# The even mixer's scan re-ordered: fronts in three pinned steps, single-step preparations, Toeplitz blocks in column tiles, and a warm-up of seven matmuls

## The chip, the cores and the metric

The kernel runs on one core of one Trainium2 chip, in one launch. The metric is the device time of a launch in microseconds; the median of several runs is compared. Times within the profile are microseconds from the start of the profiled execution, unless marked ns.

## The reference, cut to what matters

One inference step of a two-layer encoder for 512 prompt frames and 32 sample frames. Layer 0 has the even mixer, which the change is in; layer 1 (attention and gated MLP) and both convolutional feed-forward blocks are untouched.

```python
z = hn @ w_even_in                       # 1024 -> 3*512 + 512
gb, gc, xa, u = split(z)
ya = gb * causal_dwconv(gc * xa)         # part A, three taps
# part B: 32 groups of 16 channels, each with 64 complex states
bu = einsum(u, bb)                       # input into the states
hs = scan(h[t] = ab * h[t-1] + bu[t])    # complex diagonal recurrence
yb = real(einsum(hs, c)) + d * u         # states to channels, skip term
g  = gelu(yb)
yb = g * sigmoid(g @ w_glu)
y  = concat(ya, yb) @ w_even_out
```

## The kernel before

All large products are done in fp32r with each operand split into a high and a low part, so that one product is three matmuls (L131 to L133): `mm_job` issues 24 of them for one tile of 128 output columns and one half of the frames (256 or 288 columns). Weights come as 512 KB tiles: SP loads `raw` (L106), ACT makes the high part `wh` (L107), VectorE the low part `wl` (L108).

The even mixer is `mixer_even`. Its stages in order: the input norm; four tiles of the projection for `u` (evicted by `c_u`); a shuffle of `u` by 16 DMAs on SP, from frames into blocks of four frames (`UU` to `U4`, L924); then the phase of the other twelve projection tiles (`c_a`: gate, convolution input and taps, into `ya`), beside which part B runs; after it the glu (96 matmuls on `GG`), and the output projection.

Part B works on blocks of four frames, with 137 columns (`M`) for both groups of requests. Each of eight *fronts* `front(s)` takes two of the 16 state tiles: the matmuls `v` put the input into the states, VectorE rotates them with the table `E` (`rt`, then two `rg`), ACT writes the decay `cv` into a part of `sp` (L872), VectorE runs the scan (L875), rotates back (`rt`, L877) and writes the states into `sp` (L878, L879). `back(s)` multiplies the states by `Cm` (L891) and adds the products within a block through the Toeplitz blocks `Tm` (L893); ACT's gelu (L894) writes the result over `U4`. `shuffle(True, ...)` takes it back to frames, also on SP (L924). The tiles `rt`, `rg`, `sp` and `G` share four buffers (tag "pt"), so a front needs buffers that earlier fronts, backs or preparations have released. `GG` takes the buffer of `E`.

The tables are prepared meanwhile: `prep_g(ch)` makes the input table `Bm` for a chunk of four state tiles (VectorE products `gt`, ACT copies into `G`, transposes `tb`, ACT copies); `prep_c()` makes `Cm` in five portions `tau` (VectorE products, ACT copies, L794) and then zeroes `Tm`; `prep_t(ch)` makes the blocks of `Tm`: eight matmuls `tp` into 32 partitions (L837), evicted by ACT and, for the first block with the skip term `d`, by four VectorE steps (L842), and three SP DMAs (L845) that copy the block row to the other three partition groups.

The order is set by generators: `task(scan())` hands `scan`'s steps to `phase`, which after each projection tile takes two of them (`rate=2`) while evictions lag two tiles behind. Each engine then executes its instructions in the order written, except where the scheduler moves one whose operands are late; SP's loads and DMAs stand in one queue.

At the very start a warm-up of nine fp32 matmuls on zeros (L218, two passes each) runs while the first operands arrive.

Of the kernel before, what the change touches and what calls it, by code (L numbers as in the profile page):

```python
# [24 lines left out]
M = 137  # L25
# [16 lines left out]
for _n, _w in (("g_mix_pre", 16), ("g_mix_post", 16), ("g_ffn_pre", 16), ("g_ffn_post", 16),  # L42
               ("conv_a", 12), ("hist_a", 8), ("a_re", 16), ("a_im", 16),
               ("log_dt", 16), ("st_re", 16), ("st_im", 16), ("d", 16), ("b_forget", 1),
               ("g_gmlp", 4), ("conv_f", 264)):
    _pc(_n, _w)
NPRM = PC["_n"]
NPRM0 = PC["conv_f"][0]

NCST = 128 + 128 + 32  # L50

# [20 lines left out]
def trunk_kernel(ctx: ExitStack, tc: tile.TileContext, A: dict):  # L72
    nc = tc.nc
    vec, act, pool_e, pe = nc.vector, nc.scalar, nc.gpsimd, nc.tensor
# [141 lines left out]
    warm = mm.tile([128, 512], F32, tag="mm", name="warm")  # L216
    for _ in range(9):
        pe.matmul(warm[:, 0:256], zero[:, 0:1].to_broadcast([128, 128]), zero[:, 0:1].to_broadcast([128, 256]),  # L218
                  start=True, stop=True)
# [298 lines left out]
    def mixer_even(h):  # L518
        ms = ExitStack()
        s5 = ms.enter_context(tc.tile_pool(name="s5", bufs=1))  # L520
# [259 lines left out]
        def prep_c():  # L780
            ct = Tm.rearrange("p (n i a x) c -> p n i a (x c)", n=2, i=2, a=2)
            ct = ct.rearrange("p n i a (q c) -> p n i a q c", q=16)
            for tau in range(5):
                src = raw[:, 0]
                if tau:
                    t = ct[:, tau % 2]
                    for i in range(2):
                        p_ = pw[:, tau, i][:, None, :, None].to_broadcast([128, 2, 16, 16])
                        vec.tensor_tensor(t[:, i], raw[:, i], p_, op=OP.mult)
                    src = t[:, 0]  # L790
                    vec.tensor_tensor(src, src, t[:, 1], op=OP.add)
                for g in range(2):
                    s = slice(g * 64, g * 64 + 64)
                    act.activation(Cm[s, :, :, tau, g * 16:g * 16 + 16], src[s], AF.Copy)  # L794
                if tau % 2 == 0:
                    yield
            act.activation(Tm.rearrange("p q s -> p (q s)"), zero[:, 0:1].to_broadcast([128, 2048]), AF.Copy)
            yield

        g3 = {}  # L800

        def prep_g(ch):
            q0 = 4 * ch
# [9 lines left out]
            for i in range(2):  # L813
                p_ = pg[:, i, q0:q0 + 4][:, None, :, :, None].to_broadcast([128, 2, 4, 3, 16])
                b_ = bb[:, i, ch][:, :, :, None].to_broadcast([128, 2, 4, 3, 16])
                vec.tensor_tensor(t[i].rearrange("p (r q) j c -> p r q j c", r=2), b_, p_, op=OP.mult)
            vec.tensor_tensor(t[0], t[0], t[1], op=OP.add)
            for g in range(2):
                s = slice(g * 64, g * 64 + 64)
                o = G[s, :, :, 0:3, g * 16:g * 16 + 16].rearrange("p r q j c -> p (r q) j c")  # L820
                act.activation(o, t[0][s], AF.Copy)
            yield
            for r in range(2):
# [28 lines left out]
        def front(s):  # L852
# [13 lines left out]
            t4 = t.rearrange("p e r (q m) -> p e r q m", q=2)  # L866
            vec.tensor_tensor(t, v[:, None].to_broadcast([128, 2, 2, 2 * M]), e, op=OP.mult)
# [7 lines left out]
            vec.tensor_tensor_scan(g_[:, 1], cf, g_[:, 0], 0.0, op0=OP.mult, op1=OP.add)  # L875
            w_ = g_[:, 1].rearrange("p (r x) -> p r x", r=2)
            vec.tensor_tensor(t, w_[:, None].to_broadcast([128, 2, 2, 2 * M]), e, op=OP.mult)  # L877
            vec.tensor_tensor(sp[:, 0, :, 1:M + 1], t4[:, 0, 0], t4[:, 1, 1], op=OP.subtract)  # L878
            vec.tensor_tensor(sp[:, 1, :, 1:M + 1], t4[:, 0, 1], t4[:, 1, 0], op=OP.add)  # L879
# [496 lines left out]
def host_arrays(inp):  # L1376
# [142 lines left out]
```

## Time and profile before

| | before |
|---|---|
| median of 3 runs | 1392.94 us (1390.91 to 1394.11) |
| profiled execution | 1392.53 us |
| its span in the trace | 1390.8 us |
| TensorE busy | 1367.2 us, 98% |
| VectorE busy | 935.7 us, 67% |
| ScalarE (ACT) busy | 657.4 us, 47% |

The span is the part of the profiled execution that the trace shows; 1.7 us lie around it. Busy shares are means over stages that differ, so the stage of the change (28 to 156 us) is read by itself: how full each engine is there, what ended the waits of TensorE and VectorE, and in what order the last pieces of part B and of the projection come.

### The profile page before, as it was taken

How to read it: one execution, taken by the hardware profiler on the slowest of the kernel's cores; microseconds unless marked ns; L12 is line 12 of the kernel's file. 1: busy time of each engine (PE TensorE's matmuls, PEld its weight loads, DVE VectorE, ACT ScalarE, POOL GpSimd, SP SyncE). 2: the span in 40 equal slices, each digit the busy share in tenths (PEclk: the TensorE clock that was granted, in tenths of full speed). 3: DMA queues.
4: the chain of work that ended last, by engine and by line, in shares of the span. 5: the costliest groups of instructions: out<-in, count | busy, mean ns of one | idle time of the engine just before them, and what ended most of it. 6: DMA issues, size and time to landing. Idle time of an engine off the chain costs nothing.

```text
span 1390.8 us, 27437 instructions
## 1 busy us (share of the span) xinstructions
PE 1367.2 (98%) x10859; PEld 1344.2 (97%) x10859; DVE 935.7 (67%) x1968; ACT 657.4 (47%) x1314; POOL 198.3 (14%) x621
## 2 busy tenths in 40 slices
PE   8899999999999999999999999999999999999998
PEld 8798999999999999999998998999999999999998
DVE  9998738983477546868655555479843676368682
ACT  6653545543344223445547755465433343234451
POOL 1000000431022201300131100012320123013000
PEclk9999999999999999999999999999999999999999
DMA  6322352232312231331332332331223123313321
GB/s 199 94 67 63 117 184 77 77 96 72 122 62 86 97 122 39 105 113 53 99 94 70 117 109 64 108 107 62 92 92 122 46 92 107 99 50 94 100 73 50
DMA packets 49376, 128.26 MB, mean 92 GB/s; under 512 B 8368, under 2 KB 19896, under 8 KB 48992
## 3 DMA queue, kind: packets, MB, share of 16 engines
q1 hardware_dynamic: 47456, 124.35, 28.0%
q0 software_dynamic: 1792, 2.17, 0.7%
q8 instruction: 85, 1.39, 0.4%
q14 instruction: 43, 0.35, 0.1%
HBM read 116.93 MB, written 4.76 MB: 88 GB/s over the span
## 4 chain that ended last, share of the span: by engine, by line
PE 87%; DVE 8%; ACT 2%; SPq 1%; DMA 1%; issue 1%; POOL 0%; ACTq 0%; DVEq 0%
PE ps L131 27%; PE ps L133 27%; PE ps L132 27%; DVE wl L108 1%; SPq L924 1%; PE av L1254 1%; PE rp L307 1%; DVE Xl L327 1%; PE pp L1243 1%; DVE rg L875 1%; DVE rt L877 1%; ACT wh L107 1%; PE sc L1230 1%; DVE y L338 0%; DMA h<-in_x 0%
## 5 line engine op out<-in xcount | busy, mean ns | idle before, releaser
L131 PE MATMUL ps<-Xh,wh 128*128 128x256 f32 (+1 forms) x2512 | 728.1, 290 | 1.8 <-ACT wh L107 1.1
L133 PE MATMUL ps<-Xh,wl 128*128 128x256 f32 (+1 forms) x2512 | 725.5, 289 | 2.0 <-DVE wl L108 2.0
L132 PE MATMUL ps<-Xl,wh 128*128 128x256 f32 (+1 forms) x2512 | 725.6, 289 | 0.8 <-DVE Xl L327 0.5
L131 PEld LDWEIGHTS ps<-Xh,wh 128*128 128x128 f32 x2512 | 473.9, 189 | 4.4 <-ACT wh L107 1.6
L132 PEld LDWEIGHTS ps<-Xl,wh 128*128 128x128 f32 x2512 | 474.7, 189 | 3.0 <-DVE Xl L327 1.2
L133 PEld LDWEIGHTS ps<-Xh,wl 128*128 128x128 f32 x2512 | 473.0, 188 | 2.5 <-DVE wl L108 2.4
L108 DVE TENSOR_TENSOR wl<-raw,wh 128x1024 fp32r<-128x1024 f32 (+2 forms) x214 | 256.9, 1201 | 151.3 <-ACT wh L107 149.5
L107 ACT ACTIVATE wh<-raw 128x1024 fp32r<-128x1024 f32 (+2 forms) x214 | 222.1, 1039 | 248.3 <-PE ps L132 232.9
L131 PE MATMUL ps<-gh,wh 128*128 128x288 f32 (+1 forms) x704 | 203.5, 289 | 0.0
L133 PE MATMUL ps<-gh,wl 128*128 128x288 f32 (+1 forms) x704 | 203.4, 289 | 0.0
L132 PE MATMUL ps<-gl,wh 128*128 128x288 f32 (+1 forms) x704 | 202.5, 288 | 0.0
L132 PEld LDWEIGHTS ps<-gl,wh 128*128 128x128 f32 x704 | 133.5, 190 | 0.0
L131 PEld LDWEIGHTS ps<-gh,wh 128*128 128x128 f32 x704 | 133.0, 189 | 0.0
L133 PEld LDWEIGHTS ps<-gh,wl 128*128 128x128 f32 x704 | 132.9, 189 | 0.0
L278 ACT ACTIVATE t<-U,prm 128x256 f32<-128x256 f32 (+1 forms) x176 | 90.4, 517 | 71.0 <-DVE U L413 67.5
L279 DVE SCALAR_TENSOR_TENSOR t<-U,prm,t 128x256 f32<-128x256 f32 (+1 forms) x176 | 87.2, 498 | 34.9 <-ACT t L278 34.7
L413 DVE TENSOR_TENSOR U<-ps,rB 128x256 f32<-128x256 f32 (+1 forms) x176 | 76.6, 437 | 23.9 <-PE ps L133 19.8
L280 DVE SCALAR_TENSOR_TENSOR t<-U,prm,t 128x256 f32<-128x256 f32 (+1 forms) x176 | 87.5, 501 | 4.5
L416 POOL COPY hca<-U 128x2 f32<-128x2 f32 x88 | 24.3, 277 | 366.2 <-DVE U L413 366.1
L423 ACT ACTIVATE t<-t 128x288 f32<-128x288 f32 (+1 forms) x88 | 37.7, 429 | 81.6 <-DVE t L280 81.5
L439 DVE TENSOR_TENSOR y<-y,ps 128x256 f32<-128x256 f32 (+1 forms) x64 | 27.9, 436 | 62.0 <-PE ps L133 62.0
L429 ACT ACTIVATE gh<-t 128x288 fp32r<-128x288 f32 (+1 forms) x88 | 37.4, 425 | 67.3 <-DVE t L427 67.3
(272 smaller groups left out, 1376.7 us busy)
## 6 DMA issues: line engine op xcount, KB each, us to landing
raw<-in_w_up SPq DMA_DIRECT2D x88, 512.0 KB, 3.4
raw<-in_w_down SPq DMA_DIRECT2D x32, 512.0 KB, 3.4
raw<-in_w_odd_in SPq DMA_DIRECT2D x21, 512.0 KB, 3.6
raw<-in_w_gate SPq DMA_DIRECT2D x16, 512.0 KB, 4.0
raw<-in_w_even_in SPq DMA_DIRECT2D x15, 512.0 KB, 3.7
raw<-in_w_down SPq DMA_DIRECT2D x16, 384.0 KB, 3.1
raw<-in_w_even_out SPq DMA_DIRECT2D x8, 512.0 KB, 4.0
raw<-in_w_odd_out SPq DMA_DIRECT2D x8, 512.0 KB, 3.5
```

The costliest lines, as they stand in the source:

```text
L107: act.activation(wh[:, k], raw[:, k], AF.Copy)
L108: vec.tensor_tensor(wl[:, k], raw[:, k], wh[:, k], op=OP.subtract)
L131: pe.matmul(ps[:, :n], wh[:, k0 + k, :], h_, start=(i == 0), stop=False)
L132: pe.matmul(ps[:, :n], wh[:, k0 + k, :], l_, start=False, stop=False)
L133: pe.matmul(ps[:, :n], wl[:, k0 + k, :], h_, start=False, stop=(i == last))
L278: act.activation(t, v[2], AF.Copy, scale=w(2))
L279: vec.scalar_tensor_tensor(t, v[1], w(1), t, op0=OP.mult, op1=OP.add)
L280: vec.scalar_tensor_tensor(t, v[0], w(0), t, op0=OP.mult, op1=OP.add)
L413: vec.tensor_tensor(block_view(U, half)[2], like(ps, half), like(rB[half], half), op=OP.mult)
L423: act.activation(t, t, AF.Gelu_apprx_tanh)
L429: act.activation(gh[:, f - f0], g, AF.Copy)
L439: vec.tensor_tensor(yk, yk, ps, op=OP.add)
```

## The change

- The warm-up has 7 matmuls, not 9.
- `front` becomes three steps: up to `cv`; the scan and the second `rt`; the two `sp`. Its first product, the scan and the first `sp` step are pinned (`tc.keep_in_program_order`), so the scheduler keeps them where they are written, behind the evictions that were written earlier. The products of `prep_c` and `prep_g` are pinned too.
- `scan` takes the preparations from a list, one step at a time, one or two between the steps of the fronts. `prep_c` has one step for each `tau` and none of its own for the zeroing of `Tm`. `back(s - 2)` follows the scan step of front `s`; the shuffle of the first half is issued at `s == 6`; backs 6 and 7 come at the very end.
- `prep_t` puts its four matmul pairs into four column tiles of 32 columns, so that the block rows lie on 128 partitions; one VectorE step (with an identity stacked four times, `eye4`, and `d` in four columns) and one ACT copy evict them into a single buffer `ts`, and sixteen SP DMAs a chunk write `Tm`.
- The parameter table is 12 columns narrower and the constants 32 columns wider.

```diff
@@ prep_c, prep_g
-                        vec.tensor_tensor(t[:, i], raw[:, i], p_, op=OP.mult)
+                        pin(vec.tensor_tensor(t[:, i], raw[:, i], p_, op=OP.mult))
...
-                if tau % 2 == 0:
+                if tau:
                     yield
...
-            yield
+            yield True
@@ prep_t
-            for i in range(4):
-                for r in range(2):
-                    pe.matmul(ps[0:32, i * 128:i * 128 + 128], G[:, r, i],
-                              Cm[:, r, q0 + i, 0:4].rearrange("p t c -> p (t c)"), start=(r == 0), stop=(r == 1))
-            pv = ps[0:32].rearrange("p (q s) -> p q s", q=4)
-            act.activation(Tm[0:32, q0:q0 + 4, 32:128], pv[:, :, 32:128], AF.Copy)
-            for i in range(4):
-                vec.scalar_tensor_tensor(Tm[0:32, q0 + i, 0:32], ident[0:32, 0:32], P("d", q0 + i)[0:32],
-                                         pv[:, i, 0:32], op0=OP.mult, op1=OP.add)
-            for j in range(1, 4):
-                nc.sync.dma_start(Tm[j * 32:j * 32 + 32, q0:q0 + 4, j * 32:128], Tm[0:32, q0:q0 + 4, 0:128 - j * 32])
+            ts_ = s5.tile([128, 128], F32, tag="ts", name="ts")
+            for r in range(2):
+                for i in range(4):
+                    pe.matmul(ps[32 * i:32 * i + 32, 0:128], G[:, r, i],
+                              Cm[:, r, q0 + i, 0:4].rearrange("p t c -> p (t c)"), start=(r == 0), stop=(r == 1),
+                              tile_position=(0, 32 * i))
+            vec.scalar_tensor_tensor(ts_[:, 0:32], eye4, P("d", ch), ps[:, 0:32], op0=OP.mult, op1=OP.add)
+            act.activation(ts_[:, 32:128], ps[:, 32:128], AF.Copy)
+            for j in range(4):
+                for i in range(4):
+                    nc.sync.dma_start(Tm[j * 32:j * 32 + 32, q0 + i, j * 32:128],
+                                      ts_[32 * i:32 * i + 32, 0:128 - j * 32])
@@ scan
-            for s in range(10):
-                if s >= 2:
-                    back(s - 2)
-                    yield
-                if s == 5:
-                    shuffle(True, (0, 1))
-                if s < 8:
-                    front(s)
-                    yield
-                    if s == 0:
-                        yield from prep_c()
-                    if s % 2 == 0:
-                        yield from prep_t(s // 2)
-                    elif s < 5:
-                        yield from prep_g(s // 2 + 2)
+            side = [prep_c(), prep_t(0), prep_g(2), prep_t(1), prep_g(3), prep_t(2), prep_t(3)]
+            left = [0, 0, 1, 3, 5, 5, 6, 6]
...
+            for s in range(8):
+                while 7 - len(side) < left[s]:
+                    yield beside()
+                f = front(s)
+                next(f)
+                yield
+                yield beside()
+                next(f)
+                yield
                 if s >= 2:
                     back(s - 2)
-                    yield
...
+                x = beside()
+                if s == 6:
+                    shuffle(True, (0, 1))
+                yield x
+                next(f, None)
+                yield
+            while side:
+                beside()
+            back(6)
+            yield
+            back(7)
             shuffle(True, (2, 3))
```

Where the instructions stand now, at three places. The first is TensorE at the first chunk of `Tm`; `v` is the input of front 1 before and of front 2 now, `tp` the Toeplitz matmuls of chunk 0, `ps` a projection tile. Before:

```order
L133 MATMUL ps<-Xh,wl 128x288
L858 MATMUL v<-UUh,Bm 128x137 x4
L837 MATMUL tp<-Cm,g_707 32x128 x8
L131 MATMUL ps<-Xh,wh 128x256
L132 MATMUL ps<-Xl,wh 128x256
```

Changed:

```order
L133 MATMUL ps<-Xh,wl 128x288
L860 MATMUL v<-UUh,Bm 128x137 x3
L839 MATMUL tp<-Cm,g_705 32x128 x8
L860 MATMUL v<-UUh,Bm 128x137
L131 MATMUL ps<-Xh,wh 128x256
```

`tp` stands 97 rows later, behind front 1 and within front 2.

The second is SP's queue from the first shuffle on. Before:

```order
L924 DMA UUh<-UUh 32x4x137 x16
L106 DMA raw<-in_w_even_in 128x1024 x2
L845 DMA Tm<-Tm 32x4x96
L845 DMA Tm<-Tm 32x4x64
L845 DMA Tm<-Tm 32x4x32
L106 DMA raw<-in_w_even_in 128x1024
L845 DMA Tm<-Tm 32x4x96
L845 DMA Tm<-Tm 32x4x64
L845 DMA Tm<-Tm 32x4x32
L106 DMA raw<-in_w_even_in 128x1024 x2
```

Changed:

```order
L946 DMA UUh<-UUh 32x4x137 x16
L106 DMA raw<-in_w_even_in 128x1024 x4
L846 DMA Tm<-ts 32x128 x4
L846 DMA Tm<-ts 32x96 x4
L846 DMA Tm<-ts 32x64 x4
L846 DMA Tm<-ts 32x32 x4
L106 DMA raw<-in_w_even_in 128x1024 x2
L846 DMA Tm<-ts 32x32
L846 DMA Tm<-ts 32x128 x4
L846 DMA Tm<-ts 32x96 x4
L846 DMA Tm<-ts 32x64 x4
L846 DMA Tm<-ts 32x32 x3
```

Sixteen DMAs a chunk stand where three stood, and two more weight loads are ahead of the first of them.

The third is the end of part B. On TensorE, back 7 before; behind the last row shown, 152 matmuls of `c_a` follow it in all:

```order
L891 MATMUL yp<-sp,Cm 128x137
L893 MATMUL yp<-UUh,Tm 128x137
L891 MATMUL yp<-sp,Cm 128x137 x2
L893 MATMUL yp<-UUh,Tm 128x137
L132 MATMUL ps<-Xl,wh 128x288
L133 MATMUL ps<-Xh,wl 128x288
L131 MATMUL ps<-Xh,wh 128x288
```

Changed, from the last matmul of `c_a` (the first row) through backs 5, 6 and 7 to the glu:

```order
L133 MATMUL ps<-Xh,wl 128x288
L895 MATMUL yp<-sp,Cm 128x137 x2
L897 MATMUL yp<-UUh,Tm 128x137
L895 MATMUL yp<-sp,Cm 128x137 x2
L897 MATMUL yp<-UUh,Tm 128x137
L895 MATMUL yp<-sp,Cm 128x137 x2
...
L897 MATMUL yp<-UUh,Tm 128x137
L132 MATMUL ps<-GG,wh 128x274
L133 MATMUL ps<-GG,wl 128x274
```

On VectorE, the last scan before:

```order
L870 COPY rg<-prm 128x4
L941 TENSOR_TENSOR gct<-ps,rB_276 128x256
L875 SCALAR_TENSOR_TENSOR rg<-sp,rg 128x548
L877 TENSOR_TENSOR rt<-rg,E 128x1096
L878 TENSOR_TENSOR sp<-rt 128x2x137
L879 TENSOR_TENSOR sp<-rt 128x2x137
```

Changed; `wl` are the splits of two tiles of the output projection's weights, and the first `sp` row is front 6's:

```order
L979 TENSOR_TENSOR ya<-ya,t 128x288
L870 TENSOR_TENSOR rg<-rt 128x274
L871 TENSOR_TENSOR rg<-rt 128x274
L326 TENSOR_TENSOR Xl<-ya,Xh 128x288
L872 COPY rg<-prm 128x4
L108 TENSOR_TENSOR wl<-raw,wh 128x1024
L882 TENSOR_TENSOR sp<-rt 128x2x137
L108 TENSOR_TENSOR wl<-raw,wh 128x1024
L878 SCALAR_TENSOR_TENSOR rg<-sp,rg 128x548
L880 TENSOR_TENSOR rt<-rg,E 128x1096
L882 TENSOR_TENSOR sp<-rt 128x2x137
L883 TENSOR_TENSOR sp<-rt 128x2x137
```

Back 7 and the last scan moved from the middle of `c_a`'s tiles to behind the last of them.

## Rows read from the trace of the kernel before

**Rows 1.** The page, busy time of each engine over the span.

```profile
PE 1367.2 (98%) x10859; PEld 1344.2 (97%) x10859; DVE 935.7 (67%) x1968; ACT 657.4 (47%) x1314; POOL 198.3 (14%) x621
```

**Rows 2.** Windows: stretch, length, busy time by engine, clock, DMA share, GB/s.

```profile
28.00:100.00 72.00, 65.42 (x505) 63.27 (x505) 70.45 (x182) 44.65 (x88) 0.52 (x5) 0.95 0.27 78
100.00:135.10 35.10, 30.95 (x248) 29.52 (x247) 29.26 (x55) 14.10 (x34) 0.51 (x5) 1.00 0.25 71
```

**Rows 3.** Groups by line, TensorE, 28 to 156: busy, mean, idle before, releaser.

```profile
L891 PE MATMUL yp<-sp,Cm 128*128 128x137 f32 x64 | 10.5, 285 | 1.6 <-DVE sp L878 1.4
L837 PE MATMUL tp<-Cm,g 128*32 128x128 f32 x64 | 9.4, 310 | 4.5 <-ACT Cm L794 4.5
...
L893 PE MATMUL yp<-UUh,Tm 128*128 128x137 f32 x32 | 6.4, 282 | 1.8 <-DMA Tm<-Tm 1.8
L826 PE MATMUL tb<-cst,G 128*128 128x128 f32 x32 | 4.4, 280 | 2.9 <-ACT G L821 2.9
```

**Rows 4.** Windows, the stretch behind the idle time at `tp`.

```profile
66.20:70.70 4.50, 4.50 (x20) 3.56 (x21) 4.50 (x9) 3.12 (x4) 0.00 (x0) 0.50 0.08 15
```

**Rows 5.** Groups by line, VectorE, 28 to 156, shapes apart.

```profile
L108 DVE TENSOR_TENSOR wl<-raw,wh 128x1024 fp32r<-128x1024 f32 x15 | 18.3, 1220 | 1.0 <-ACT wh L107 1.0
...
L868 DVE TENSOR_TENSOR rg<-rt 128x274 f32<-128x274 f32 x8 | 3.5, 436 | 1.0 <-PE tb L826 0.9
...
L842 DVE SCALAR_TENSOR_TENSOR Tm<-cst,prm,tp 32x32 f32<-32x32 f32 x16 | 3.1, 228 | 0.0
...
L953 DVE TENSOR_TENSOR ya<-ps,rB 128x288 f32<-128x288 f32 x3 | 1.4, 456 | 2.0 <-PE ps L133 2.0
```

**Rows 6.** Timeline of VectorE: start, duration, instruction, idle before.

```profile
131.67 1.28 DVE L875 TENSOR_TENSOR_SCAN rg<-sp,rg 128x548 f32<-128x548 f32 x1
...
134.68 0.44 DVE L879 TENSOR_TENSOR sp<-rt 128x274 f32<-128x274 f32 x1
...
145.82 0.73 DVE L978 TENSOR_TENSOR GG<-UUh,GG 128x548 fp32r<-128x548 f32 x1 [1.56 <-DMA out_o_ssm<-so]
```

**Rows 7.** Timeline of TensorE at `tp`, at the glu's two ends, at L1272.

```profile
66.19 3.62 PE L837 MATMUL tp<-Cm,g 128*32 128x128 f32 x16 [4.48 <-ACT Cm L794]
...
156.05 0.28 PE L131 MATMUL ps<-GG,wh 128*128 128x274 f32 x1
...
168.25 0.28 PE L131 MATMUL ps<-Xh,wh 128*128 128x256 f32 x1
...
837.42 0.69 PE L1272 MATMUL sc<-kS,qT 64*32 64x288 f32 x8
838.04 0.39 PE L131 MATMUL ps<-Xh,wh 128*128 128x256 f32 x1
```

**Rows 8.** Timeline of ACT: back 7's gelu, the first copy of the shuffled rows.

```profile
136.71 0.40 ACT L894 ACTIVATE UUh<-yp 128x274 f32<-128x274 f32 x1 [1.08 <-PE yp L893]
...
145.13 0.66 ACT L977 ACTIVATE GG<-UUh 128x548 fp32r<-128x548 f32 x1 [3.21 <-DMA UUh<-UUh]
```

**Rows 9.** Timeline of SP's queue: issue of DMAs, merged rows with their count.

```profile
72.25 1.88 SPq L845 DMA_DIRECT2D Tm<-Tm  x3
...
132.02 10.31 SPq L924 DMA_DIRECT2D UUh<-UUh  x16
...
154.20 0.34 SPq L968 DMA_DIRECT2D out_o_conva<-co  x1
```

**Rows 10.** Timeline of TensorE at the start: the first and the eighth real matmul.

```profile
7.21 0.47 PE L131 MATMUL ps<-Xh,wh 128*128 128x256 f32 x1
...
8.47 0.39 PE L132 MATMUL ps<-Xl,wh 128*128 128x256 f32 x1
```

**Rows 11.** Waits of VectorE, 28 to 136: total, times, longest.

```profile
DVE rg L875 <- ACT sp L872: 3.2, 3, 2.2
```

**Rows 12.** Line L845: waits of SP ahead of `Tm` DMAs, ns min/median/max.

```profile
L845 SPq EVENT_SEMAPHORE  x4: 17/4172/9695, 69.6 to 120.0; - x4
```

**Rows 13.** The page, DMA issues by line: KB each, us to landing.

```profile
raw<-in_w_even_out SPq DMA_DIRECT2D x8, 512.0 KB, 4.0
```

More of the change, by code (lines that the diff above doesn't have):

```diff
@@ L43 @@
                ("conv_a", 12), ("hist_a", 8), ("a_re", 16), ("a_im", 16),
-               ("log_dt", 16), ("st_re", 16), ("st_im", 16), ("d", 16), ("b_forget", 1),
+               ("log_dt", 16), ("st_re", 16), ("st_im", 16), ("d", 4), ("b_forget", 1),
                ("g_gmlp", 4), ("conv_f", 264)):
@@ L48 @@
 NPRM0 = PC["conv_f"][0]
-NCST = 128 + 128 + 32
+NCST = 128 + 128 + 32 + 32
 def units():
@@ L210, in trunk_kernel @@
     mask_s = cst[:, 256:288]
+    eye4 = cst[:, 288:320]
     ones = const.tile([128, 1], F32, tag="ones", name="ones")
@@ L216, in trunk_kernel @@
     warm = mm.tile([128, 512], F32, tag="mm", name="warm")
-    for _ in range(9):
+    for _ in range(7):
         pe.matmul(warm[:, 0:256], zero[:, 0:1].to_broadcast([128, 128]), zero[:, 0:1].to_broadcast([128, 256]),
@@ L788, in prep_c @@
                         p_ = pw[:, tau, i][:, None, :, None].to_broadcast([128, 2, 16, 16])
-                        vec.tensor_tensor(t[:, i], raw[:, i], p_, op=OP.mult)
+                        pin(vec.tensor_tensor(t[:, i], raw[:, i], p_, op=OP.mult))
                     src = t[:, 0]
-                    vec.tensor_tensor(src, src, t[:, 1], op=OP.add)
+                    pin(vec.tensor_tensor(src, src, t[:, 1], op=OP.add))
                 for g in range(2):
@@ L794, in prep_c @@
                     act.activation(Cm[s, :, :, tau, g * 16:g * 16 + 16], src[s], AF.Copy)
-                if tau % 2 == 0:
+                if tau:
                     yield
             act.activation(Tm.rearrange("p q s -> p (q s)"), zero[:, 0:1].to_broadcast([128, 2048]), AF.Copy)
-            yield
         g3 = {}
+        pin = tc.keep_in_program_order
         def prep_g(ch):
@@ L815, in prep_g @@
                 b_ = bb[:, i, ch][:, :, :, None].to_broadcast([128, 2, 4, 3, 16])
-                vec.tensor_tensor(t[i].rearrange("p (r q) j c -> p r q j c", r=2), b_, p_, op=OP.mult)
-            vec.tensor_tensor(t[0], t[0], t[1], op=OP.add)
+                pin(vec.tensor_tensor(t[i].rearrange("p (r q) j c -> p r q j c", r=2), b_, p_, op=OP.mult))
+            pin(vec.tensor_tensor(t[0], t[0], t[1], op=OP.add))
             for g in range(2):
@@ L866, in front @@
             t4 = t.rearrange("p e r (q m) -> p e r q m", q=2)
-            vec.tensor_tensor(t, v[:, None].to_broadcast([128, 2, 2, 2 * M]), e, op=OP.mult)
+            pin(vec.tensor_tensor(t, v[:, None].to_broadcast([128, 2, 2, 2 * M]), e, op=OP.mult))
             vec.tensor_tensor(g[:, 0], t4[:, 0, 0], t4[:, 1, 1], op=OP.add)
@@ L873, in front @@
             pool_e.memset(sp[:, 0:2, :, 0:1], 0.0)
+            yield
             g_ = g.rearrange("p (x r) i m -> p x (r i m)", x=2)
-            vec.tensor_tensor_scan(g_[:, 1], cf, g_[:, 0], 0.0, op0=OP.mult, op1=OP.add)
+            pin(vec.tensor_tensor_scan(g_[:, 1], cf, g_[:, 0], 0.0, op0=OP.mult, op1=OP.add))
             w_ = g_[:, 1].rearrange("p (r x) -> p r x", r=2)
             vec.tensor_tensor(t, w_[:, None].to_broadcast([128, 2, 2, 2 * M]), e, op=OP.mult)
-            vec.tensor_tensor(sp[:, 0, :, 1:M + 1], t4[:, 0, 0], t4[:, 1, 1], op=OP.subtract)
+            yield
+            pin(vec.tensor_tensor(sp[:, 0, :, 1:M + 1], t4[:, 0, 0], t4[:, 1, 1], op=OP.subtract))
             vec.tensor_tensor(sp[:, 1, :, 1:M + 1], t4[:, 0, 1], t4[:, 1, 0], op=OP.add)
@@ L899, in scan, with beside @@
             yield from prep_g(1)
-            for s in range(10):
+            side = [prep_c(), prep_t(0), prep_g(2), prep_t(1), prep_g(3), prep_t(2), prep_t(3)]
+            left = [0, 0, 1, 3, 5, 5, 6, 6]
+            def beside():
+                while side:
+                    try:
+                        return next(side[0])
+                    except StopIteration:
+                        side.pop(0)
+            for s in range(8):
[7 more added lines that the diff above has]
+                yield
                 if s >= 2:
                     back(s - 2)
-                    yield
-                if s == 5:
+                x = beside()
+                if s == 6:
                     shuffle(True, (0, 1))
-                if s < 8:
-                    front(s)
-                    yield
-                    if s == 0:
-                        yield from prep_c()
-                    if s % 2 == 0:
-                        yield from prep_t(s // 2)
-                    elif s < 5:
-                        yield from prep_g(s // 2 + 2)
+                yield x
+                next(f, None)
+                yield
+            while side:
+                beside()
+            back(6)
+            yield
+            back(7)
             shuffle(True, (2, 3))
@@ L1449, in host_arrays @@
     put("st_im", gp(f["state_ssm_im"][0, 0]))
-    put("d", np.tile(f["s5_d"][0].reshape(16, 32).T, (4, 1)))
+    put("d", f["s5_d"][0].reshape(4, 128).T)
     prm[:8, PC["b_forget"][0]] = f["b_forget"][0]
@@ L1459, in host_arrays @@
     cst[:, 256:288] = np.where(j[None, :] <= (i % 32)[:, None], 0.0, NEG)
+    cst[:, 288:320] = np.tile(np.eye(32), (4, 1))
     A["cst"] = cst
```

## The prediction

> **What bounds the kernel now.** Over the whole span TensorE is busy 98% [rows 1], so a reader would look for TensorE stalls only. The even mixer's middle is different. VectorE leaves 1.55 us free between 28 and 100 us and 5.85 between 100 and 135.1, 7.4 us of 107 [rows 2]: there it is as full as TensorE. TensorE's own losses in this stretch are named by the groups of its lines: 4.5 us before `tp` (waiting for ACT's copies into `Cm`), 2.9 before `tb` (ACT's copies into `G`), 1.8 before the `Tm` matmuls of a back (a DMA) and 1.6 before the `sp` matmuls of a back: 10.8 us [rows 3]. The idle time at `tp` has a second price: the granted clock is 0.50 in the 4.5 us after it [rows 4], so half of that, 2.2 us, is lost too. About 13 us is therefore what this change can work on.
>
> The other thing to see is the end of the stage. The sum for back 7 is ready when VectorE's last `sp` ends, at 134.68 + 0.44 = 135.1 [rows 6]. I call this time T1. TensorE then still has 152 matmuls of c_a, up to 156.05, where the first glu matmul starts [rows 7]. Below them lies a whole chain: gelu of back 7, eight shuffle DMAs, their landing at 145.13, which is T1 + 10.0, and then the copies of `GG` [rows 8, 9]. Nobody waits for it.
>
> **The change part by part.** *Warm-up.* Two fp32 matmuls are four passes, none longer than the 0.47 us of the first real matmul, so this one, now at 7.21, could start at most 1.9 us earlier. But the eighth real matmul starts at 8.47, where seven steps of 0.12 would put it at 8.05: its `Xl` comes from VectorE only then [rows 10]. What starts earlier waits there. I take 0; bounds −1.9 and 0, the first only if `Xl` came earlier too, which no edit does.
>
> *Column tiles.* Each `tp` is 16 passes. At the halved clock they took 3.62 us [rows 7], so 0.113 each at full clock, 1.8 us a chunk and 7.2 us in four. No column tiling of this shape is in the trace; the nearest is L1272, eight 64x32 tiles whose matmuls take 0.62 us from 837.42 to the next matmul at 838.04 [rows 7], or 0.078 each. Sixteen would take 1.24, so 0.56 less, 2.2 us in four chunks. Bounds: 0 (no overlap) and 5.4 (four at a time at the old pace, 0.45 a chunk). I take 2.2, the row's own pace.
>
> The Trainium skill, page TensorEngine Tiling (Array Packing), section Overview, gives up to 4x for a small dimension of at most 32, and by that the saving would be the 5.4 us. The trace here shows 8 tiles in 0.62 us, which is some 1.4 times the old pace for each, so I stay with the row.
>
> *Evictions of `tp`.* Sixteen 32x32 steps become four of 128x32, and ACT reads four times the partitions in the same time. The sixteen cost 16 x 0.228 = 3.6 us of VectorE [rows 5]; four wider ones, at most 0.46 each as an eviction of 288 columns, 1.8. The gain of 1.8 or more is in VectorE's sum below.
>
> *The DMAs.* Twelve `Tm` DMAs become 64, sixteen a chunk, and all stand in SP's queue, in front of raw weight loads and of the shuffle. The price of one is not in the trace. DMAs between SBUF tiles with several runs per partition go at 10.31 / 16 = 0.64 us; those with one run per partition, to DRAM, take 0.34 [rows 9]. The new ones have one run per partition on both sides, so I take the lower with the same 0.05 between two: 0.39, or 6.2 us a chunk. The other end is 0.64, or 10.3 us a chunk; the second rival works with it.
>
> *The order.* This is the part that decides. Before, 152 c_a matmuls followed back 7. Now the last c_a tile stands ahead of backs 5, 6 and 7, and VectorE's order ahead of the last scan holds the evictions and taps of c_a's last tiles and five more weight splits. So T1 now comes after the end of c_a, not before it. I work out T1 by TensorE and then by VectorE.
>
> TensorE: 156.05, less 10.8 for the stalls, less 2.2 for the clock, less 2.2 for the tiles, less three backs that now come later. A back is 12 passes at the 0.11 of above, 1.3 us, three 3.9. That leaves 136.95, say 137.0, for the end of c_a if TensorE never waited. From there VectorE has to do, in this order, one eviction, a multiply and an `Xl` (0.46 each, all of that size), two `rg` (0.87), a weight split (1.22), one `sp` (0.44), a second split (1.22), then scan, `rt` and two `sp` (3.45, from 131.67 to 135.12) [rows 5, 6]: 8.6 us by the means, and about 8.2 since starts overlap a little. So **T1 = 145.2 + W**, where W is all waiting of TensorE up to the end of c_a and of VectorE behind it.
>
> What is left of the waits? `tb` still waits for ACT's `G` three times (2.9 as now). `tp` and the `Tm` matmuls are further from what they wait for, and I let them go. New is that the scan of a front needs ACT's `cv`, which needs the back of two fronts earlier for its buffer, and now stands closer behind it; the 0.9 for this is an estimate, between 0 and the 2.2 that this wait takes at its longest now [rows 11]. W = 3.8, T1 = 149.0. VectorE's own sum agrees: the steps that now stand ahead of T1 and did not before are 5 splits (6.1 us), 8 `Xl`, 3 evictions and 3 multiplies into `ya`, 4 evictions into `XC` and `gct` and 6 taps (24 of about 0.46, 11.0), less 1.8: 15.3, and some 13.5 with starts that overlap as above by up to 0.08 in each of the 29; 135.1 + 13.5 = 148.6 with the same 7.4 us of idle.
>
> *The tail.* After T1, TensorE does back 7 (1.3), then 24 glu matmuls (12.2 / 96 = 0.127 each between 156.05 and 168.25, so 3.05) and 24 of the output projection (0.12 each, 2.85): it is busy to T1 + 7.2. The shuffled rows are there at T1 + 10.0; the high half of `GG` takes ACT 0.66 and the low half VectorE 0.73 [rows 6, 8], so it goes on at about T1 + 11, with smaller waits behind, 3.9 us in all. Then all that is left is what followed 156.05 before. So the end moves by T1 + 1.3 + 3.9 − 156.05 = **T1 − 150.85**. With 149.0 this is −1.85 us. TensorE also idles some 6 us before T1 while backs 6 and 7 wait; 4.5 us of idle at 61.7 was followed by a clock of 0.50 [rows 4, 7]. Slow work before T1 + 11 is hidden by the wait for `GG`, a second fall behind it is not: 0 to 2.2, I take 1. Sum: −0.9 us against the profiled 1392.5 us (span 1390.8), that is 1391.6. The median of the runs shown is 0.4 above the profiled one, so **1392.0 us**.
>
> **The rivals.** *1. The interleaving does what it says.* ACT's `Cm` and `G` are ready, `tb` no longer waits, W is 0 to 2. With 0 and no clock loss: 145.2 − 150.85 = −5.65, 1387.3; with tiles four at a time 3.2 less. For it: 5.85 of the 7.4 us of VectorE's idle lie in one stage [rows 2], behind single waits that an order can remove. Against it: TensorE and VectorE have the same floor, and two full engines seldom wait for nothing. I give 1387.
>
> *2. SP's queue becomes the bound (slower).* At 0.64 us the 64 DMAs take 41 us. SP must issue them, 16 shuffle DMAs (10.3) and six weight loads (3.8 if none takes longer) between the zeroing of `Tm` and the load for the output projection whose split stands right ahead of the last scan on VectorE. The first `Tm` DMA goes at 72.25 now [rows 9]; `prep_c` is spread over some three more tiles of 2.9 us (24 matmuls of 0.12), so from 81: 136 if SP never waited. It waits for each chunk's `ts`; in front of the `Tm` DMAs it waits four times now, 0.02 to 9.7 us with a median of 4.2 [rows 12], 18 in all. Between 0 and 18 I take 12: the load is issued at 148, lands 4.0 us later [rows 13], and its split, a second one and the last scan with its `rt` and `sp` take 5.9 us: T1 = 158, +7, 1400 to 1402 with the clock. It decides from about 0.5 us for one DMA. For it stand the shuffle's DMAs at 0.64, against it the single-run one at 0.34 [rows 9].
>
> The Trainium skill, page DMA: Bandwidth & Descriptors, section Rules for kernel authors, speaks for this rival: many small transfers should be coalesced, and transfers under 64 KB mostly pay overhead. The rows agree in so far as 16 DMAs take 10.31 us of SP's time; whether the shorter ones cost as much no row shows.
>
> *3. The waits only change place (slower).* With the 10.8 us of stalls in other places, W = 10.8 and T1 = 156: +5.15, 1398 to 1399 with the clock. The place is the pairing of ACT's `cv` with the backs. It is slower than before once W passes 4.7. Against it: `Cm` is now built in one-step portions.
>
> **How the numbers follow.** Chances: forecast 0.35, rival 1 0.33, rival 2 0.17, rival 3 0.15. The forecast's own range is 1389 to 1395.5 (W from 1.5 to 6, clock 0 to 2.2). The range to 1385 and 1402 leaves out the better half of the tiles in rival 1 (0.08) and the worst of rivals 2 and 3 (0.10). A measurement of this kernel can tell about 0.2%, 2.8 us, from no change. Faster by more: rival 1 and 0.04 of the forecast, 0.37; slower by more: rivals 2 and 3 and 0.02, 0.34; the same 0.29.
>
> **What would show it.** In the new profile: T1 (the end of the last `sp`) near 149, c_a's last matmul near 140, the `Tm` DMAs at 0.39 apart, sixteen `tp` passes in 1.2 us, and TensorE waiting about 4 us for `GG`. T1 below 146 is rival 1. `Tm` DMAs at 0.64 and VectorE waiting for a weight load ahead of the last scan is rival 2. TensorE stalls of over 8 us ahead of c_a's end is rival 3. The prediction would be wrong in kind if the time moved elsewhere, after 200 us.

## The result: 13 us slower, by the second rival

The changed kernel takes 1405.3 us (median of 5 runs, 1404.36 to 1407.09) against 1391.97 us of the kernel before in the same job: a ratio of 1.0097, 95% interval 1.0082 to 1.0111. The forecast was 1392.0 with a range up to 1402; the time lies outside it, and 3 us above the 1400 to 1402 that the second rival gave. The profiled execution has a span of 1403.6 us, 12.8 more than the 1390.8 before. Of these, 11.2 are there when the first feed-forward matmul on `gh` starts: at 332.62 in place of 321.46. The loss is made in the even mixer; another 1.5 us shows between 725 and 753 us, where the code is the same and the clock is granted at 0.50 for 3.4 us in this profile and not in that of before. It was not studied.

The page's first section of the changed kernel, in the columns of [rows 1]: TensorE is busy 1.5 us less than before, and yet the span is longer.

```profile
PE 1365.7 (97%) x10855; PEld 1342.7 (96%) x10855; DVE 933.3 (66%) x1956; ACT 654.1 (47%) x1314; POOL 197.6 (14%) x621
```

The waits of TensorE in the first 260 us (engine, line, for whom: total, times, longest). The 4.5 us at `tp` [rows 3] have become 0.9. In their place stand 11.6 us at the backs, for VectorE's `sp`, and 4.4 us at the glu.

```profile
PE yp L895 <- DVE sp L882: 11.6, 2, 10.3
PE ps L131 <- ACT GG L999: 4.4, 1, 4.4
PE tb L827 <- ACT G L822: 3.0, 3, 1.2
...
PE ps L131 <- DVE XC L968: 1.8, 1, 1.8
...
PE tp L839 <- ACT Cm L795: 0.9, 1, 0.9
```

Who holds `sp` back is read from three timelines (start, duration, instruction, idle before it and for whom). SP first, which answers to [rows 9]:

```profile
103.89 11.14 SPq L846 DMA_DIRECT2D Tm<-ts  x16
115.12 0.53 SPq L106 DMA_DIRECT2D raw<-in_w_glu  x1
116.81 10.75 SPq L846 DMA_DIRECT2D Tm<-ts  x16
127.66 0.53 SPq L106 DMA_DIRECT2D raw<-in_w_glu  x1
128.23 1.28 SPq L946 DMA_DIRECT2D UUh<-UUh  x2
129.67 10.64 SPq L846 DMA_DIRECT2D Tm<-ts  x16
140.36 9.00 SPq L946 DMA_DIRECT2D UUh<-UUh  x14
149.46 1.00 SPq L106 DMA_DIRECT2D raw<-in_w_even_out  x2
```

From 103.89 to 150.46 the queue has gaps of 1.7 us in all. The output projection's first weight load goes at 149.46, because the last two chunks' `Tm` DMAs, a glu load and 16 shuffle DMAs stand right ahead of it. ACT gets the weights 3.9 us later:

```profile
153.38 1.06 ACT L107 ACTIVATE wh<-raw 128x1024 fp32r<-128x1024 f32 x1 [4.27 <-DMA raw<-in_w_even_out]
154.34 0.38 ACT L898 ACTIVATE UUh<-yp 128x274 f32<-128x274 f32 x1
```

The second row is the gelu of back 5, whose matmuls were issued by 145.50: it stands behind the split on ACT, and so does the `cv` of the last front. And VectorE, which answers to [rows 6]:

```profile
149.57 0.17 DVE L872 COPY rg<-prm 128x4 f32<-128x4 f32 x1
154.47 1.22 DVE L108 TENSOR_TENSOR wl<-raw,wh 128x1024 fp32r<-128x1024 f32 x1 [4.74 <-ACT wh L107]
155.61 0.43 DVE L882 TENSOR_TENSOR sp<-rt 128x274 f32<-128x274 f32 x1
155.97 1.22 DVE L108 TENSOR_TENSOR wl<-raw,wh 128x1024 fp32r<-128x1024 f32 x1
157.30 1.30 DVE L878 TENSOR_TENSOR_SCAN rg<-sp,rg 128x548 f32<-128x548 f32 x1
158.64 1.30 DVE L880 TENSOR_TENSOR rt<-rg,E 128x1096 f32<-128x1096 f32 x1
159.97 0.44 DVE L882 TENSOR_TENSOR sp<-rt 128x274 f32<-128x274 f32 x1
160.33 0.44 DVE L883 TENSOR_TENSOR sp<-rt 128x274 f32<-128x274 f32 x1
```

VectorE is idle for 4.74 us in front of a weight split that nobody needs yet; front 6's `sp` and the last scan stand behind it. T1, the end of the last `sp`, is 160.77. On TensorE the backs show it; in the last row four such matmuls take 1.25 us instead of 0.63, at half the clock:

```profile
145.04 0.63 PE L895 MATMUL yp<-sp,Cm 128*128 128x137 f32 x4
145.50 0.40 PE L897 MATMUL yp<-UUh,Tm 128*128 128x137 f32 x2
156.19 1.25 PE L895 MATMUL yp<-sp,Cm 128*128 128x137 f32 x4 [10.29 <-DVE sp L882]
```

The windows say the same of the clock (columns as in [rows 2]; the seventh figure is the granted clock): 0.50 for the 10.2 us in which TensorE has 3 us of work.

```profile
149.00:159.20 10.20, 3.01 (x12) 2.78 (x12) 5.31 (x8) 3.60 (x7) 0.10 (x1) 0.50 0.56 170
```

### The profile page after: what moved, and what is told of

It reads as the page before. It is cut to its first block, busy times and chain, and to the rows that moved or that the text cites. A ratio compares the mean times of both kernels' runs of the same rounds, so it can differ in the third digit from the quotient of the medians.

```text
span 1403.6 us, 27500 instructions
## 1 busy us (share of the span) xinstructions
PE 1365.7 (97%) x10855; PEld 1342.7 (96%) x10855; DVE 933.3 (66%) x1956; ACT 654.1 (47%) x1314; POOL 197.6 (14%) x621
## 4 chain that ended last, share of the span: by engine, by line
PE 84%; DVE 8%; SPq 3%; ACT 2%; DMA 2%; issue 1%; POOL 0%; DVEq 0%; ACTq 0%
PE ps L131 27%; PE ps L133 27%; PE ps L132 26%; SPq L846 2%; DVE wl L108 2%; PE av L1276 1%; SPq L946 1%; PE rp L308 1%; PE pp L1265 1%; DMA raw<-in_w_even_out 1%; PE sc L1252 1%; ACT wh L107 0%; DVE Xl L328 0%; DMA h<-in_x 0%; DVE rt L880 0%
```

## The experiments

After the result I had one theory and one rival. **Queue**: the 64 `Tm` DMAs cost SP some 0.69 us each on average (11.06 us for the first sixteen), and what stands behind them makes T1 late. **Order**: the c_a steps that now stand ahead of the last scan make T1 late by themselves, whatever the DMAs cost.

### Undo the Toeplitz part, or do it alone

`e1_old_toeplitz`: the changed kernel with the old `prep_t`.

```diff
-            for j in range(4):
-                for i in range(4):
-                    nc.sync.dma_start(Tm[j * 32:j * 32 + 32, q0 + i, j * 32:128],
-                                      ts_[32 * i:32 * i + 32, 0:128 - j * 32])
+            for j in range(1, 4):
+                nc.sync.dma_start(Tm[j * 32:j * 32 + 32, q0:q0 + 4, j * 32:128], Tm[0:32, q0:q0 + 4, 0:128 - j * 32])
```

> The changed kernel with the old preparation of the Toeplitz blocks (32 partitions, three SP DMAs a chunk, 12 in all), everything else of the change kept. Theory queue (64 DMAs at 0.69 us fill SP's queue, and the weight load behind them holds the last scan): the end of the last sp comes back from 160.8 to 149 or so and the time to 1390 to 1396. Rival order (the steps of c_a ahead of the last scan cost the time, whatever the DMAs): 1400 or more, with the last sp near 158. The scheduler also puts one weight split ahead of the last scan here instead of two.

Measured: 1394.7 us, 1.0020 of before (1.0011 to 1.0030). 10.6 of the 13.3 us are gone. T1 is not at 149, though:

```profile
151.78 0.44 DVE L882 TENSOR_TENSOR sp<-rt 128x274 f32<-128x274 f32 x1
```

`e2_new_toeplitz_alone`: the kernel before with the new `prep_t`, `eye4` and the narrow `d`.

> The kernel before with the new preparation of the Toeplitz blocks alone (column tiles, 64 DMAs, narrower d). Theory queue: Tm lands late for the backs and the weight loads stand behind it, 3 to 10 us slower than before (1395 to 1402). Rival order: the tiles save some 5 us of TensorE and the DMAs hide behind it, 1388 to 1392.

Measured: 1396.1 us, 1.0032 (1.0020 to 1.0044). The part costs 4 us in the old order as well, although it saves TensorE time there. The largest wait is for late `Tm` (1.8 us in [rows 3], x32 as there):

```profile
L895 PE MATMUL yp<-UUh,Tm 128*128 128x137 f32 x32 | 7.3, 319 | 5.6 <-DMA Tm<-ts 5.6
```

It is not all of it: behind the glu TensorE waits 2.2 us for ACT's copies into `Xh`, where it waited 0.6 before, and e2's runs have a lower granted clock than those of before beside them (a mean of 0.992 against 0.997).

### Keep the DMAs and take them, or what stands behind them, off SP

`e3_tm_gpsimd` changes one word, `nc.sync` into `nc.gpsimd`, for the 64 `Tm` DMAs.

> The changed kernel with its 64 Tm DMAs issued by GpSimd, so that SP's queue holds none of them. Theory queue: SP is free, the output projection's loads go early, the last sp ends near 150 and the time is 1390 to 1397, if GpSimd issues one in 0.5 us as it does for B and KA. Rival order: 1400 or more.

Measured: 1395.0 us, 1.0024 (1.0015 to 1.0034). GpSimd issues sixteen in 8.05 us, 0.50 each (timeline of GpSimd):

```profile
83.17 8.05 POOL L846 DMA_DIRECT2D Tm<-ts  x16 [11.90 <-DVE ya L975]
```

`e4_out_loads_gpsimd` leaves all 64 on SP and moves only two loads:

```diff
-                nc.sync.dma_start(raw[:, k], A[name][idx][:, k])
+                q_ = nc.gpsimd if name == "w_even_out" and idx < 2 else nc.sync
+                q_.dma_start(raw[:, k], A[name][idx][:, k])
```

> The changed kernel with the first two weight loads of the output projection issued by GpSimd instead of SP, all 64 Tm DMAs left on SP. It takes away only the wait of the split ahead of the last scan. Theory queue, by that load: the last sp ends near 153.6 and the time is near 1398. If the late Tm (and not the load) is what costs, no change, 1403 to 1407.

Measured: 1397.2 us, 1.0041 (1.0026 to 1.0056). Two loads out of SP's queue give back 8.1 us of the 13.3. So most of the loss is one wait at the head of a queue, which everything behind it shares: a weight load behind the DMAs on SP, and its split ahead of the last scan on VectorE. In e1, e3 and e4 the scheduler also puts one split, not two, ahead of that scan (1.2 us), so the comparison is not of the wait alone.

`e11_split_dmas` measures the price by itself: the kernel before, each `Tm` DMA cut into four with one run per partition.

```diff
-                nc.sync.dma_start(Tm[j * 32:j * 32 + 32, q0:q0 + 4, j * 32:128], Tm[0:32, q0:q0 + 4, 0:128 - j * 32])
+                for i in range(4):
+                    nc.sync.dma_start(Tm[j * 32:j * 32 + 32, q0 + i, j * 32:128], Tm[0:32, q0 + i, 0:128 - j * 32])
```

> The kernel before with each of its Tm DMAs cut into four with one run per partition (48 instead of 12), nothing else changed: the price of the disputed DMAs by itself. Theory queue: SP issues them 0.65 to 0.70 us apart as it does the longer ones, 12 a chunk take 8 us instead of 1.9, and the time is 3 to 8 us above before. My prediction's price of 0.39 us would make it 1391 to 1394.

Measured: 1393.6 us, 1.0014 (1.0004 to 1.0024). Of my range of 3 to 8 us above before, 1.7 came, and by the time alone a price of 0.39 would pass as well. The price stands in SP's timeline, and it is the point in dispute: 8.56 / 12 = 0.71 us in the first chunk (0.63 to 0.72 in the four), where three took 1.88, or 0.63 each, in [rows 9].

```profile
73.76 8.56 SPq L846 DMA_DIRECT2D Tm<-Tm  x12
```

The single DMAs show what the average hides (SP's DMAs into `Tm`, shortest, median and longest in ns; the kernel before, then the changed one):

```profile
L845 SPq DMA_DIRECT2D Tm<-Tm x12: 586/593/912, 72.2 to 127.0; - x12
...
L846 SPq DMA_DIRECT2D Tm<-ts x64: 512/589/1716, 82.7 to 139.7; - x64
```

The median did not change: 0.59 us, 0.64 with the 0.05 between two. One DMA in each chunk of the changed kernel took 1.2 to 1.7 us, and that makes the average 0.67 to 0.70. Why one is long was not studied.

### What is left over: 3 us

Without the DMAs' cost the changed order is still 3 us behind. Not all of this need be order: in e1's profile the first matmul on `gh` is only 1.3 us late, and the runs of e1 have a mean granted clock of 0.9952 against 0.9966 for those of before beside them. The difference, taken over 1392 us, is 2 us at most (an estimate, as if it all fell on time in which TensorE had work). No run separates the two. **Tail** was the first theory for this: behind T1, TensorE waits 7.0 us for `GG` in e1, since c_a is used up. **Pins**: the pinned steps hold others back.

`e5_rate3_old_toeplitz` is e1 with `rate=3` in c_a's phase, so that 100 matmuls of c_a stand behind back 7 again. `e6_rate3_tm_gpsimd` is the same with e3's DMAs. `e8_before_rate3` is the control: the kernel before with `rate=3`.

> The changed kernel with the old Toeplitz preparation and three steps of part B after each projection tile instead of two, so that 100 matmuls of c_a stand behind back 7 again. Theory tail (what was left over in e1, 2.8 us above before, is the uncovered chain from the last sp to the shuffled rows): TensorE's wait for GG, 7.0 us in e1, is gone and the time is 1385 to 1390. Rival pins (the pinned fronts hold the evictions of c_a back, wherever they stand): 1393 or more, with new waits of TensorE for evictions.

> As e5, but with the column tiles kept and their 64 DMAs on GpSimd. Theory tail: 1384 to 1390, by the tiles up to 5 us of TensorE less than e5 if TensorE bounds the stage. If the DMAs from GpSimd come too late for the backs that now stand earlier: TensorE waits for Tm, 1392 or more.

> The kernel before with three steps of part B after each projection tile instead of two. A control for e5: if the rate alone brings the gain, this is as fast as e5; my theory is that the old order had no uncovered tail, so nothing is gained there, and that the earlier fronts hold evictions back, 1391 to 1397.

Measured: e5 1395.2 us, 1.0021 (1.0011 to 1.0031); e6 1392.7 us, 1.0005 (0.9995 to 1.0015); e8 1393.9 us, 1.0016 (1.0006 to 1.0025). The wait for `GG` did go from e5's list of waits, which is led by

```profile
PE tb L827 <- ACT G L822: 3.1, 3, 1.9
PE ps L133 <- DVE wl L108: 2.7, 3, 1.6
PE tp L838 <- ACT Cm L795: 2.2, 1, 2.2
PE v L859 <- DVE rt L868: 2.1, 4, 0.7
```

and the time stayed. T1 is 143.2 there, but the first glu matmul starts at 157.6, 1.6 later than before: TensorE waits earlier, for the fronts' tables, instead of later, for `GG`. The tail theory fell: covering it brought nothing in e5. The rival of that expectation, new waits for evictions, is not what the list shows either. e6 is 2.5 us below e5, about half of what its column tiles save TensorE (4.6 us, below), and 2 us nearer to before than e3, though the intervals of the two just touch; no wait for `Tm`, its rival's sign, is in its list.

`e10_no_pins` is e1 with `pin = lambda x: x`.

> As e1 (the changed kernel with the old Toeplitz preparation, 1394.7), without the pins on the fronts' and preparations' VectorE steps. Theory pins (the pins cost, since a pinned step waits behind an eviction that is itself late): 1390 to 1393. If the order of the generators' steps is what the rest of the loss comes from: the same as e1, 1393 to 1397.

Measured: 1396.0 us, 1.0034 (1.0022 to 1.0046). The pins cost nothing; without them it is, if anything, 1 us worse, and TensorE waits 3.8 us once for an eviction (`gct`).

`e7_warm7` is the kernel before with `range(7)` for the warm-up.

> The kernel before with a warm-up of 7 matmuls instead of 9 and nothing else. My theory: what starts earlier waits for Xl, so no change, 1391 to 1393. Rival: the shorter warm-up brings the clock down in the first 30 us, 1393 to 1395.

Measured: 1391.9 us, 1.0005 (0.9995 to 1.0015): no difference. TensorE's timeline answers to [rows 10]. The first real matmul starts 0.59 us earlier, at 6.62, the eighth 0.25 us earlier, with 0.39 us of waiting for the same `Xl`. A lower clock, the rival's sign, does stand in this profile (0.66 from 13 to 18 us), but it does not follow the warm-up: e17 below, with nine matmuls, has 0.58 from 14 to 18, and e1, with seven, has 1.00 in all of its first 28 us.

```profile
6.62 0.47 PE L131 MATMUL ps<-Xh,wh 128*128 128x256 f32 x1
...
8.22 0.39 PE L132 MATMUL ps<-Xl,wh 128*128 128x256 f32 x1 [0.39 <-DVE Xl L327]
```

### Which engine does the time follow?

My prediction took TensorE and VectorE for equally full up to T1. Four runs take work off one of them, in the old order and in that of e1, and so leave out part of the result. `e13_before_less_dve` and `e15_e1_less_dve` drop the line `vec.tensor_tensor(yv, yv, t, op=OP.mult)`; `e14_before_less_pe` and `e16_e1_less_pe` use `range(K - 1)` in eight of c_a's tiles.

> The kernel before without the last multiply of part A (the convolution's result into ya; 8 VectorE steps, 2.8 us at their pace; part A's output is then the gate alone). Theory two full engines (in the even mixer VectorE bounds the stage up to the last sp): 1 to 3 us less than before, 1389 to 1391. Rival (TensorE alone bounds it, its waits are the only loss): within 1 us of before.

> The kernel before with 7 instead of 8 pieces of the contraction in eight of c_a's twelve tiles (48 matmuls less, 6.0 us of TensorE; those projections miss an eighth of their sum). If TensorE bounds the stage: 6 us less, 1386. Theory two full engines: only a part comes through, 2 to 4 us, since behind the last sp TensorE alone works and before it VectorE does.

> e1 (the changed order with the old Toeplitz preparation, 1394.7) without the last multiply of part A, as in e13. Theory: the last sp stands behind all of c_a's evictions here, so VectorE's 2.8 us come through in full, 1391.5 to 1392.5. Rival (TensorE bounds it): 1394 to 1395.

> e1 with 48 matmuls of c_a less, as in e14 (6.0 us of TensorE). Theory: TensorE already waits 7 us for GG behind the last sp, so little comes through, 0 to 3 us, 1392 to 1395. Rival (TensorE bounds it): 1388.7.

| work taken off | old order | order of the change (e1, 1394.7) |
|---|---|---|
| VectorE, 2.8 us | e13 1390.97: 1.0 us less, 0.9991 (0.9982 to 1.0000) | e15 1394.83: 0.1 us more |
| TensorE, 6.0 us | e14 1385.96: 6.0 us less, 0.9954 (0.9942 to 0.9967) | e16 1392.91: 1.8 us less |

In the old order the time follows TensorE, in full; the 1.0 us of e13 lies at the edge of both its theory and its rival, and its interval reaches 1.0000. In the new one it follows neither engine by itself: 6 us less of TensorE bring 1.8, 2.8 less of VectorE nothing. What is left as a bound there is the chain that passes between engines, from front to scan, `sp`, back, gelu, the shuffle's DMAs and `GG`, whose last part lies open behind c_a. That this chain is it was not shown by a run that shortens it alone. My theory of two equally full engines is refuted for the new order by e15, and for the old by e14, where it allowed 2 to 4 us.

### Two attempts to build Tm without DMAs

`e9_toeplitz_on_pe` (order of e5) and `e12_before_toeplitz_on_pe` (old order) let TensorE write all block rows into 128 partitions through column tiles, over a diagonal that GpSimd has put into `Tm`.

```diff
+            pool_e.tensor_tensor(Tm, ident[:, None, :].to_broadcast([128, 16, 128]),
+                                 P("d", 0, 16)[:, :, None].to_broadcast([128, 16, 128]), op=OP.mult)
...
+                pe.matmul(ps[:, i * 128:i * 128 + 128], ident, Tm[:, q0 + i], start=True, stop=False)
+                for r in range(2):
+                    for j in range(4):
+                        pe.matmul(ps[32 * j:32 * j + 32, i * 128 + 32 * j:i * 128 + 128], G[:, r, i],
+                                  Cm[:, r, q0 + i, 0:4 - j].rearrange("p t c -> p (t c)"), start=False, stop=(r == 1),
+                                  tile_position=(0, 32 * j))
+            act.activation(Tm[:, q0:q0 + 4].rearrange("p q s -> p (q s)"), ps, AF.Copy)
```

> As e5 (three steps a tile), but Tm is built without any DMA: TensorE writes all four block rows of a chunk through column tiles into 128 partitions, on top of a diagonal matrix with d that GpSimd has written into Tm, and one ACT copy of 128x512 evicts it. Theory queue: no DMA and no VectorE step is left for Tm, 1384 to 1391. If GpSimd's product takes longer than the zeroing by ACT did, the first tp waits for it: 1393 or more.

> The kernel before, its order kept, with Tm built on TensorE as in e9 and no DMA. Theory: the 1.8 us of waiting for Tm's DMA and 2 us of VectorE go, the 4.5 us in front of tp and the clock behind it stay or grow if GpSimd's product is slow: 1387 to 1392.

Measured: e9 1408.3 us, 1.0117 (1.0100 to 1.0134); e12 1399.6 us, 1.0059 (1.0044 to 1.0074). e9's list of TensorE waits is led by the wait that its expectation had named as its risk, and GpSimd's product takes 5.1 us in e9 and 3.6 in e12 where ACT's zeroing took 1.9. Both are misses as designs, and the 16 us of e9 are more than this wait. e12's list is led by 5.5 us for VectorE's `ya`, at an eviction. The rest was not followed up in either.

```profile
PE tp L838 <- POOL Tm L798: 9.2, 1, 9.2
```

### The tiles in the old order, on two queues

If TensorE bounds the old order, the part of the change that saves TensorE time should pay there, once its DMAs are spread. `e17_tiles_two_queues` is e2 with this loop; `e18_tiles_tp_later` adds that the first chunk's `tp` is written behind front 1 and pinned.

```diff
+            for i in range(4):
+                for j in range(4):
+                    q_ = nc.gpsimd if i % 2 else nc.sync
+                    q_.dma_start(Tm[j * 32:j * 32 + 32, q0 + i, j * 32:128],
+                                 ts_[32 * i:32 * i + 32, 0:128 - j * 32])
```

> The kernel before, its order kept, with the column tiles and their 64 DMAs split between two queues by state tile: tiles 0 and 2 of a chunk on SP, 1 and 3 on GpSimd, the pair that the first back needs first. Theory (TensorE bounds the old order, e14; a Tm DMA costs its queue 0.7 us): the tiles' 4.6 us of TensorE come through and the DMAs land in time, 1386 to 1389; against e2 (all on SP, 1396) the queue alone is changed. If Tm still lands late for the backs: 1391 or more, with waits of yp for Tm.

> e17 with the first chunk's tp written behind front 1 and pinned there, so that one projection tile of 24 matmuls stands where TensorE waited 4.5 us for Cm. Theory (TensorE bounds the old order): up to 4.5 us of waiting and the 2.2 us of slow clock behind it less than e17, 1381 to 1387. Rival (VectorE, full between 60 and 80 us, only passes the wait on to the next eviction): as e17.

Measured: **e17 1385.6 us, 0.9963 (0.9950 to 0.9975)**, faster than both kernels; e18 1387.7 us, 0.9974 (0.9963 to 0.9985). Sixteen DMAs of a chunk now take 6.1 us instead of 11, and the wait for `Tm` is 2.5 us against 5.6 in e2 (timelines of SP and of TensorE, group of lines):

```profile
72.56 6.08 SPq L847 DMA_DIRECT2D Tm<-ts  x8
67.79 0.64 PE L839 MATMUL tp<-Cm,g 128*32 128x128 f32 x16 [4.47 <-ACT Cm L795]
L896 PE MATMUL yp<-UUh,Tm 128*128 128x137 f32 x32 | 7.0, 303 | 2.5 <-DMA Tm<-ts 2.5
```

In e18 the 4.5 us at `tp` are gone, and a longer wait for VectorE stands at an eviction:

```profile
PE ps L131 <- DVE ya L958: 5.5, 1, 5.5
```

So this wait was VectorE's lateness, and TensorE's order only chooses where it shows. That is the rival of e18's expectation; at 2 us above e17, with intervals that overlap, e18 is no faster.

## Why the prediction was wrong, step by step

**The price of a `Tm` DMA: the step that failed.** I took 0.39 us, by the one row with a single run per partition (0.34, to DRAM), against the 0.64 of the shuffle's row. Measured is an average of 0.67 to 0.70 (10.64 to 11.14 us for sixteen) and, in e11, 0.63 to 0.72. The nearer rows were the shuffle's and one that I passed over, the old `Tm` DMAs themselves: 1.88 us for three in [rows 9]. Both go from SBUF to SBUF between 32 partitions, as the new ones do, and the number of runs was the wrong likeness. The upper end of my range, 0.64, is what most of them cost; the long one in each chunk comes on top. Rival 2 gave the mechanism in full, with the queue, the load, the split ahead of the last scan, a load issued at 148 and T1 = 158; measured are 149.46 and 160.77. I gave it 0.17, and a point of decision of 0.5 us. The rule that I had beside it, of the Trainium skill, page DMA: Bandwidth & Descriptors, section Rules for kernel authors (coalesce many small transfers), was the better guide here, and the runs agree with it: 10.6 us between the changed kernel and e1, and 1.7 in e11, where only the cutting is new. What was lost here is issue time on SP and the place in its queue.

**T1 = 145.2 + W.** W came out at 15.6, not 3.8. The part up to the end of c_a is 7.3 (the first matmul of back 5 starts at 144.34 against 137.0). TensorE's waits from 28 to 144.5 us add up to 7.6: 3.0 for `tb` (2.9 was right), 1.8 for `XC`, 1.2 for ACT's `ts`, 0.9 for `tp`, 0.7 in two small ones; all but the first I had left out (over 8 was to be the sign of rival 3). The clock took another 3.4 (0.59 granted from 22 to 26 us, 0.84 and 0.73 in the two 4 us from 78 to 86), which I had put at nothing ahead of T1, and the tiles gave back 2.4 more than I took off. That makes 8.6; the difference of 1.3 stays open. The part behind is 8.3: 4.74 is the wait for the split, the rest an `rt`, two taps and three `Xl` that I had ahead of this point.

In e1, with the queue free, c_a ends at 143.7. That is 137.0, with 2.2 more because e1 has no column tiles and 4.5 of waits (2.8 for `tb`, 0.9 for `tp`, 0.8 in two small ones). T1 is 152.22, 8.5 us behind it. This is near the 8.2 that I worked out, but partly by luck, as other steps stand there: one split and one `sp` less, two taps and three `Xl` more.

**The end moves by T1 − 150.85: right.** It held in four kernels; the last two columns are the shift by the formula and the start of the first feed-forward matmul against before.

| kernel | T1 | T1 − 150.85 | measured shift |
|---|---|---|---|
| the change | 160.77 | +9.9 | +11.2 |
| e4, two loads moved | 154.16 | +3.3 | +3.8 |
| e1, old Toeplitz | 152.22 | +1.4 | +1.3 |
| e3, DMAs on GpSimd | 151.48 | +0.6 | +1.5 |

The predicted wait for `GG` was 3.9 us with smaller ones behind; 4.4 was measured. The clock fell in the tail, as weighed: 0.50 from 149.0 to 159.2, and again after the wait for `GG`, for 3.4 us (1.7 us lost, where I had taken 1).

**Column tiles: the right sign, half the size.** Sixteen passes take 0.65 us, not 1.24:

```profile
77.17 0.65 PE L839 MATMUL tp<-Cm,g 128*32 128x128 f32 x16 [0.94 <-ACT Cm L795]
```

Against 1.8 at full clock before, four chunks save 4.6 us and not 2.2. L1272's tiles have 288 columns against 128 here; my row was too far away. The Trainium skill, page TensorEngine Tiling (Array Packing), section Overview, with its up to 4x gave 5.4 us, and the trace agrees better with it than with my row. In the changed order the saving is not seen in the time (e3 against e1), as TensorE waits behind c_a; with `rate=3` about half is (e6 against e5). In the old order it is: e17.

**Warm-up at nothing: right** (e7). **The wait at `tp` and the clock behind it: gone, as forecast** (0.9 of 4.5), but what it was worth was wrong. I had it as 6.7 us of TensorE that come back as time. In e18 it came back as another wait.

**The forecast of no change** was near what is left without the queue (e1 and e3, 3 us above before, inside my range), with T1 2.5 to 3.2 us later there than mine. The miss is the queue.

## What to carry to other kernels

Before cutting a DMA into several, multiply their number by the issue time of the nearest DMA with the same two memories and a similar partition count, and add up what that queue then holds; anything behind it, a prefetch above all, is late by that sum, and a split of a prefetched weight that stands early in a compute engine's order hands the delay to work that doesn't need it. When a stall is removed, ask which engine made it: TensorE's wait for a full VectorE moves, while work taken off the engine that bounds the stage (six of six microseconds in the old order) comes back as time. A part of a bundle can be worth having by itself: here the column tiles, in the old order and with their DMAs on two queues, make the kernel 0.4% faster.

## What the runs showed of the hardware that I had not expected

- The SBUF-to-SBUF DMAs of SP cost the same when they are smaller: 0.64 us from one to the next for 34 KB [rows 9] and for most of 4 to 16 KB. Long ones of 1.2 to 1.7 us come in between, and averages over a chunk go from 0.62 to 0.76 (e17). GpSimd issued the same ones in 0.50 us.
- Four column tiles of 128x32 run so well side by side that sixteen passes with 128 columns took 0.65 us, with weight loads of 0.106 to 0.110 us each, as long as untiled ones of that shape.
- Queued work at half clock cost little: of the 10.2 us at 0.50, TensorE was busy 3.0.
